# Second branch projection: eight of its sixteen k-tiles as seven products for eight, and two modulation blocks summed by matmuls

## The chip, the cores and the metric

The kernel runs on one core of a Trainium2 chip. The metric is the time of one execution on the device in microseconds (us), the median of several runs; a profile records one more execution, instruction by instruction. The engines are named as in the profile: PE (TensorE, matmuls), PEld (its weight loads), DVE (VectorE), ACT (ScalarE), POOL (GpSimd) and SP (the queue that issues most DMAs).

## The reference, cut to what matters

One layer of a streaming encoder over T = 576 tokens (512 of a prompt, 64 of a sample). What the change touches:

```
mod = (silu(c) @ w_ada + b_ada)                    # 6 blocks of 1024, here cut into 12 of 512 ("u" 0 to 11)
sh1, sc1, gt1, sh2, sc2, gt2 = split(mod, 6)
...
y = group RMSNorm of the Mamba branch              # 576 x 2048
mixed = (g_attn * (o_attn @ w_branch_attn) + g_ssm * (y @ w_branch_ssm)) @ w_out
x = x + gt1 * mixed
h2 = rms_normalize(x) * g_norm_ffn * (1.0 + sc2) + sh2
```

The weights w_branch_attn and w_out are 1024 x 1024, w_branch_ssm is 2048 x 1024, w_ada is 1024 x 6144; all is float32.

## The kernel before

Everything is written once as a list of operations; a planner then places them, engine by engine, by its own table of durations, latencies and a model of the DMA queue, with priorities (`R.prio`), extra caution for matmuls (`R.slack`) and explicit "not before" edges (`R.after`). What it emits is a fixed order per engine, so an engine whose next instruction is not ready waits, whatever stands behind it.

Activations are kept as [128 channels, tokens], and a projection is done for one column tile `a` of 128 outputs at a time. To keep float32 accuracy each operand is split in two: `h` (rounded) by an ACT copy and `l` (the rest) by a DVE subtraction, and each product is three matmuls, wh·yh, wh·yl, wl·yh. One matmul covers 288 tokens (`TH`, half of T). `fm` therefore issues 8 k-tiles x 3 x 2 halves = 48 matmuls for 1024 inputs.

The weights come through `fetch`: a DMA of 512 KB into a `raw` buffer (two of them), then the split into `wh` and `wl` (three slots each). `specs` is the list of weight tiles in the order of use; `getw` takes the next one and lets `fetch` run ahead.

The stage that the change rewrites follows the scan of the Mamba branch. First the attention branch, `pba0` to `pba7` (operands `oh`, `ol`), while the last groups of the scan still run; its gated results go to the DRAM tensor `m_d`. Then the second branch, `pbs0` to `pbs7`: 16 k-tiles `yh`, `yl`, read back from `y_d` through `stage` buffers (`load_split`), 96 matmuls a column tile. Each result is gated (`g`), added to the attention part (`m`, read from `m_d`) and split into `mh`, `ml`. Then comes the output projection `pwo`, on `mh`, `ml`.

Beside this DVE computes modulation blocks 5 to 9 as filler (`ada_columns`): for each block the weights come in four DMAs of 512 KB (tile `adr`), and 32 DVE operations of 512 columns each multiply them by silu(c) and add them up in two accumulators `aacc`, one for the prompt and one for the sample. `ada_sum` then sums over the partitions by 8 small matmuls (`pick`, 32 columns of weights, in four column groups), and `ada_out` turns the result and stores it in `modc`. The blocks of the kernel's very first stage are done another way (`ada_pair`): there the weights go straight through PE, 32 small matmuls a block, `sil` (silu(c)) being the stationary operand. Blocks 10 and 11 come later and stay as they are but for the place of block 10's sum.

The feed-forward projections further on already use the scheme of seven products for eight (Strassen's, in Winograd's form), so the words T1 to T4 (differences of weight quarters) and S1 to S4 (differences of activation quarters) also occur there.

Of the kernel before, what the change touches and what calls it, by code (L numbers as in the profile page):

```python
# [5 lines left out]
F32 = mybir.dt.float32  # L6
F32R = mybir.dt.float32r
# [241 lines left out]
class Plan:  # L249
# [10 lines left out]
    def __init__(self, tc):  # L260
        self.tc, self.nc = tc, tc.nc
        self.ops, self.events, self.offset, self.slack, self.also = [], [], 0, SLACK, []
        self.vec, self.act, self.pool, self.pe, self.sync = (Engine(self, e) for e in ("vector", "scalar", "gpsimd", "tensor", "sync"))
# [25 lines left out]
    def add(self, eng, fn, args, kw):  # L289
# [20 lines left out]
        op.dur, op.dur_dma = self.cost(op, outs, ins)  # L310
        self.ops.append(op)
# [240 lines left out]
def build(tc, I, O):  # L552
# [62 lines left out]
    queue = []  # L615
    state = {"ld": 0, "sp": 0, "get": 0}
    raws, outs, outs_made = {}, {}, []
# [9 lines left out]

    def fetch(done, limit=1 << 30):

        while len(outs_made) < len(specs):  # L630
            i = len(outs_made)
            outs_made.append(i)
            queue.extend((i, s) for s in specs[i])
            outs[i] = []
        with R.prio(4000 if done else 0):
            more = True
            while more:
                more = False
                j = state["ld"]
                if j < min(len(queue), limit) and j < state["sp"] + NRAW:  # L640
                    i, s = queue[j]
                    if s == "misc":
# [4 lines left out]
                    else:  # L647
                        raws[j] = (load_raw(*s), s[1], s[2], 27 <= j < 48)
# [3 lines left out]
                if j < min(state["ld"], limit) and (j < NWH or queue[j - NWH][0] < done):  # L652
                    outs[queue[j][0]].append(split(*raws.pop(j)))
                    state["sp"] += 1
                    more = True
# [87 lines left out]
    def ada(u, pl, bufs):  # L743

        p = px(f"pada{u}", "py")
        raws = [pl.tile([P, 2, 512], F32, name=f"wada{u}_{k2}", tag="adr", bufs=bufs) for k2 in range(4)]
        loads = [sync.dma_start(raw, w_ada[256 * k2:256 * k2 + 256, 512 * u:512 * u + 512].rearrange("(k p) n -> p k n", p=P))
                 for k2, raw in enumerate(raws)]
        with R.after(loads[-1:]):
            for kt in range(8):  # L750
                for g in range(4):
                    pe.matmul(p[32 * g:32 * g + 32, 0:P], sil[:, kt, :], raws[kt // 2][:, kt % 2, P * g:P * g + P],
# [1505 lines left out]
```

## Time and profile before

| | us |
|---|---|
| median of 3 runs (1356.64 to 1356.99) | 1356.81 |
| the profiled execution | 1357.67 |
| span of its instructions, first start to last end | 1355.7 |

The profiled execution lies 1.97 us above its own span and 0.86 us above the median of the runs. A row of a timeline has the start, the time covered, the engine, the operation, what it writes and reads, and a count of equal instructions in a row; in brackets stands the idle time before it and what ended it. A matmul's row lasts longer than the distance to the next start, because matmuls overlap, so costs on PE are read from starts. A plain float32 matmul, as the small ones of the modulation are, leaves two records each, so x16 is 8 of them and x32 is 16.

### The profile page before, as it was taken

To read this page: it belongs to the slowest core of one execution; us is meant where nothing else is said; L and a number is where in the kernel's file an instruction comes from. 1 tells how busy PE (TensorE), PEld (TensorE's weight loads), DVE (VectorE), ACT (ScalarE), POOL (GpSimd) and SP (SyncE) were. 2 spreads that over 40 slices of the span, in tenths; PEclk is the share of its full clock that TensorE was granted. 3 is DMA by queue.
4 is the path that set the end of the run, shared out by engine and by line. 5 is a ranking of instruction groups with operands and counts; after the bars stand their busy time and mean duration, and the time that the engine had idled before them with its cause. 6 is when DMAs were issued, how large, how long until landed. Compare 5 with 4: busy or idle time off the path is not lost.

```text
span 1355.7 us, 27900 instructions
## 1 busy us (share of the span) xinstructions
PE 1341.3 (99%) x10677; PEld 1306.5 (96%) x10677; DVE 1141.8 (84%) x2307; ACT 754.1 (56%) x1593; POOL 245.4 (18%) x377
## 2 busy tenths in 40 slices
PE   7999999999999999999999999999999999999998
PEld 6999999999999999999999999999999999999998
DVE  5788999887778798888887688867799999878897
ACT  5445333777777666666565342225476666665453
POOL 2312011230310235545463300001000000000000
PEclk9999999999999999999999999999999999999999
DMA  9762435574755464454445698747423343325352
GB/s 302 226 181 83 111 107 156 124 186 106 173 136 123 131 180 115 113 150 128 131 124 172 209 294 253 232 141 246 127 87 101 96 131 102 94 74 141 98 164 63
DMA packets 267877, 200.31 MB, mean 148 GB/s; under 512 B 25488, under 2 KB 239616, under 8 KB 267744
## 3 DMA queue, kind: packets, MB, share of 16 engines
q1 hardware_dynamic: 263056, 183.40, 46.3%
q0 software_dynamic: 4400, 15.00, 5.4%
q8 instruction: 83, 1.36, 0.4%
q14 instruction: 50, 0.41, 0.1%
q10 hardware_dynamic: 288, 0.13, 0.0%
HBM read 157.75 MB, written 28.96 MB: 138 GB/s over the span
## 4 chain that ended last, share of the span: by engine, by line
PE 91%; DVE 5%; DMA 1%; issue 1%; ACT 1%; POOL 1%; SPq 0%; DVEq 0%; POOLq 0%; ACTq 0%
PE mm L544 63%; PE py L544 16%; PE px L544 12%; DVE score L544 1%; DVE m L544 1%; DMA raw<-in_w_in 1%; DVE wl L544 1%; DMA bc<-acs_d 0%; DMA B<-in_w_down 0%; SPq L544 0%; DVE tok L544 0%; DVE xs L544 0%; ACT wh L544 0%; DVE rr L544 0%; ACT wl L544 0%
## 5 line engine op out<-in xcount | busy, mean ns | idle before, releaser
L544 ACT ACTIVATE wh<-raw 128x1024 fp32r<-128x1024 f32 (+3 forms) x144 | 140.6, 979 | 172.5 <-PE mm L544 131.6
L544 PE MATMUL mm<-hTl,wh 128*128 128x288 f32 (+1 forms) x1024 | 232.6, 302 | 1.1 <-DVE hTl L544 1.1
L544 PE MATMUL mm<-hTh,wh 128*128 128x288 f32 (+1 forms) x1024 | 231.2, 303 | 0.6 <-ACT wh L544 0.5
L544 PE MATMUL mm<-hTh,wl 128*128 128x288 f32 (+1 forms) x1024 | 230.0, 302 | 0.0
L544 PEld LDWEIGHTS mm<-hTl,wh 128*128 128x128 f32 (+1 forms) x1024 | 166.7, 188 | 4.1 <-DVE hTl L544 1.8
L544 PEld LDWEIGHTS mm<-hTh,wh 128*128 128x128 f32 (+1 forms) x1024 | 165.7, 188 | 3.8 <-ACT wh L544 0.7
L544 PEld LDWEIGHTS mm<-hTh,wl 128*128 128x128 f32 (+1 forms) x1024 | 165.4, 188 | 1.6 <-issue 0.9
L544 DVE TENSOR_TENSOR wl<-raw,wh 128x1024 fp32r<-128x1024 f32 (+2 forms) x99 | 122.1, 1235 | 27.1 <-ACT wh L544 26.0
L544 POOL DMA_DIRECT2D wl<-raw x23 | 20.9, 907 | 471.2 <-PE px L544 312.9
L544 DVE SCALAR_TENSOR_TENSOR cu<-xc,wc,cu 128x579 f32<-128x579 f32 x96 | 83.3, 868 | 2.0 <-ACT cu L544 1.0
L544 PE MATMUL mm<-wh,hTl 128*128 128x256 f32 x256 | 73.2, 286 | 0.0
L544 PE MATMUL mm<-wl,hTh 128*128 128x256 f32 x256 | 72.5, 284 | 0.0
L544 PE MATMUL mm<-wh,hTh 128*128 128x256 f32 x256 | 72.4, 285 | 0.0
L544 DVE SCALAR_TENSOR_TENSOR aacc<-adr,sil,aacc 128x512 f32<-128x512 f32 x84 | 59.0, 751 | 5.0 <-DMA adr<-in_w_ada 4.9
L544 PE MATMUL mm<-yh,wl 128*128 128x288 f32 x256 | 55.2, 296 | 0.0
L544 PE MATMUL mm<-yh,wh 128*128 128x288 f32 x256 | 55.0, 296 | 0.0
L544 PE MATMUL mm<-yl,wh 128*128 128x288 f32 x256 | 54.9, 296 | 0.0
L544 PE MATMUL mm<-xhS,wh 128*128 128x290 f32 (+1 forms) x248 | 54.8, 296 | 0.0
L544 ACT ACTIVATE P<-lg,mn 128x128 f32<-128x128 f32 (+4 forms) x72 | 41.7, 580 | 22.6 <-DVE mn L544 21.3
L544 ACT ACTIVATE dec<-dec,nacs 128x128 f32<-128x128 f32 x128 | 42.4, 393 | 15.9 <-POOL dec L544 15.9
L544 PE MATMUL mm<-xhS,wl 128*128 128x290 f32 (+1 forms) x232 | 51.2, 296 | 0.0
L544 PEld LDWEIGHTS mm<-wh,hTl 128*128 128x128 f32 x256 | 48.3, 189 | 0.4
(565 smaller groups left out, 4071.7 us busy)
## 6 DMA issues: line engine op xcount, KB each, us to landing
raw<-in_w_in SPq DMA_DIRECT2D x80, 512.0 KB, 4.2
adr<-in_w_ada SPq DMA_DIRECT2D x36, 512.0 KB, 5.4
raw<-in_w_gate_up SPq DMA_DIRECT2D x22, 512.0 KB, 3.8
wl<-raw POOLq DMA_DIRECT2D x21, 512.0 KB, 4.7
rawu<-in_w_gate_up SPq DMA_DIRECT2D x20, 512.0 KB, 3.9
bc<-acs_d SPq DMA_DIRECT2D x32, 256.0 KB, 3.7
raw<-in_w_branch_ssm SPq DMA_DIRECT2D x16, 512.0 KB, 4.7
gate_d<-sg SPq DMA_DIRECT2D x16, 288.0 KB, 2.2
```

Of the source, the lines that this page charges most:

```text
L544: getattr(engines[x.eng], x.fn)(*[real(a) for a in x.args], **{k: real(v) for k, v in x.kw.items()})
```

## The change

For k-tiles 0 to 7 of the second branch, the 1024 x 256 weights of two neighbouring column tiles (a pair `r`) and the activations are cut into quarters of 512: B11, B21 (first column tile, k-tiles 0 to 3 and 4 to 7) and B12, B22 (second), A11, A12 (first half of the tokens, k-tiles 0 to 3 and 4 to 7) and A21, A22 (second half). Seven products of 4 k-tiles x 3 = 12 matmuls take the place of eight; they accumulate in banks x, y, z, with copies on ACT and additions on DVE in between. K-tiles 8 to 15 stay as they were (the "plain" part, two column tiles of 48 matmuls a pair). New work on DVE and ACT: the four weight differences of a pair, the four activation differences once, splits of quarters (512 columns of weights, 1152 of activations) in place of whole tiles. Buffers: a pair's two raw tiles stay until their last difference is taken; the plain weights get a `rawp` buffer of their own; S3, S1, A22 and S4 are split into the space of `oh` and `ol` once the attention projection has read them.

Modulation blocks 5 and 6 go through PE as in `ada_pair` (`ada_direct`): four clusters of 16 small matmuls from three `adr` buffers. Blocks 7 to 9 stay on DVE. The gated result is added to `m_d` by an accumulating DMA of POOL's queue for all eight column tiles (`a >= 8` never holds), and `ml` of the first six tiles is made by an ACT copy of -mh and an accumulating DMA.

```diff
@@ fetch @@
+                    if quad is not None and free(tag):
+                        r, q = quad
+                        if n - 2 in raws:
+                            x, y = (raws.pop(n - 2 + k)[0] for k in range(2))
+                            pair_raws[r] = {"B11": x[:, 0:4], "B21": x[:, 4:8], "B12": y[:, 0:4], "B22": y[:, 4:8]}
+                        src = quad_source(r, sum_pool[0], q)
+                        t = wp.tile([P, 8, P], F32R, name=f"wq{q}{r}", tag=tag, bufs=NWH)
+                        act.activation(t[:, 0:4], src, AF.Copy)
+                        vec.tensor_tensor(t[:, 4:8], src, t[:, 0:4].bitcast(F32), OP.subtract)
...
-    for a in range(8):
-        fm_spec(I["w_branch_ssm"][0], P * a, 0)
-        fm_spec(I["w_branch_ssm"][0], P * a, 1024)
+    SSM_ORDER = ((1, 2, 6, 7, 5, 4, 3),) + ((1, 7, 6, 2, 5, 4, 3),) * 3
+    SSM_QUADS = {1: ("B11", "A11"), 2: ("B21", "A12"), 6: ("T2", "S2"), 7: ("T3", "S3"), 5: ("T1", "S1"), 4: ("T4", "A22"), 3: ("B22", "S4")}
+    for r in range(4):
+        pair_spec(I["w_branch_ssm"][0], r, [SSM_QUADS[p][0] for p in SSM_ORDER[r]])
+        for a in (2 * r, 2 * r + 1):
+            fm_spec(I["w_branch_ssm"][0], P * a, 1024)
+            specs[-1][0] += (True,)
...
+    def ada_direct(u, pl, bufs):
+
+        p = px(f"padc{u}", "py")
+        with R.prio(4000):
+            R.slack = 3.0
+            for k4 in range(2):
+                raws = [pl.tile([P, 2, 512], F32, name=f"wada{u}_{k4}{i}", tag="adr", bufs=bufs) for i in range(2)]
...
+                with R.after(loads):
+                    for i in range(4):
+                        for g in range(4):
+                            pe.matmul(p[32 * g:32 * g + 32, 0:P], sil[:, 4 * k4 + i, :], raws[i // 2][:, i % 2, P * g:P * g + P],
...
-    with R.prio(-2000):
-        for u in range(4 + NADX + NADA, 10):
-            ada_columns(u, adv)
...
+    with R.prio(-2000):
+        for u in range(4 + NADX, 10):
+            if u in (5, 6):
+                ada_direct(u, adv, 3)
+            else:
+                ada_columns(u, adv, bank="py", bufs=3)
...
-        ps = fm(f"pbs{a}", getw(2), lambda k: yh[k], lambda k: yl[k])
-        vec.scalar_tensor_tensor(t2(g), t2(g), 1.0, ps, op0=OP.add, op1=OP.mult)
-        vec.tensor_tensor(m, m, g, OP.add)
...
+        if a in mixed:
+            vec.tensor_tensor(g, g, mixed[a], OP.add)
+        else:
+            pool.dma_start(g, m_d[:, a, :], accum_op=OP.add)
...
+        for p in SSM_ORDER[r]:
+            (hi, lo), = getw()
+            o, (yh_q, yl_q), starts = bank["y" if p == 2 else "z" if p in (7, 4) else "x"], yq[SSM_QUADS[p][1]], p in (1, 2, 7)
+            for k in range(4):
+                for w, y in ((hi, yh_q), (hi, yl_q), (lo, yh_q)):
+                    pe.matmul(o, w[:, k], y[:, k], start=(starts and k == 0 and w is hi and y is yh_q), stop=(k == 3 and w is lo),
+                              skip_group_check=not starts)
+            with R.prio(4000):
+                if p in (1, 6, 7):
+                    act.activation({1: acc0[:, :TH], 6: acc0[:, TH:], 7: acc1}[p], o, AF.Copy)
+                if p == 5:
+                    vec.tensor_tensor(acc1, acc1, o, OP.add)
```

Three places show what the planner made of it. In the rows below a name ends in the buffer's number; `mm`, `px`, `py` are PSUM banks.

PE, where the attention projection ends and the second branch begins, before: whole k-tiles, both halves of the tokens in a row.

```order
L544 MATMUL mm_0_114<-ol7_0_5061,wh_1_102 128x288 x2
L544 MATMUL mm_0_114<-oh7_0_5053,wl_1_105 128x288 x2
L544 MATMUL mm_1_115<-yh0_0_9045,wh_2_103 128x288 x2
L544 MATMUL mm_1_115<-yl0_0_9061,wh_2_103 128x288 x2
L544 MATMUL mm_1_115<-yh0_0_9045,wl_2_106 128x288 x2
```

The same engine now, from the end of the first product (A11) on: five matmuls of the product on S3 (in the space of `oh0`), the first of the product on A12, then the second cluster of modulation block 5 (`adr`, 16 small matmuls), then A12 again.

```order
L545 MATMUL mm_1_115<-ylA11_0_9075,wh_2_103 128x288
L545 MATMUL mm_1_115<-yhA11_0_9074,wh_2_103 128x288
L545 MATMUL px_0_112<-oh0_0_5046,wl_0_104 128x288 x5
L545 MATMUL mm_0_114<-yhA12_0_9076,wl_2_106 128x288
L545 MATMUL py_0_110<-adr_2_9050,sil_0_119 32x128 x8
L545 MATMUL py_0_110<-adr_0_9048,sil_0_119 32x128 x8
L545 MATMUL mm_0_114<-ylA12_0_9077,wl_2_106 128x288
L545 MATMUL mm_0_114<-yhA12_0_9076,wl_2_106 128x288 x2
```

So PE's queue now holds matmuls that need a DMA of `w_ada` to have landed, where only DVE needed it before.

PE, some 40 matmuls into the output projection, before: column tile 0 runs through k-tiles 6 and 7, then column tile 1 begins.

```order
L544 MATMUL mm_1_115<-mh6_0_9334,wl_0_104 128x288 x2
L544 MATMUL mm_1_115<-mh7_0_9335,wh_0_101 128x288 x2
L544 MATMUL mm_1_115<-ml7_0_9343,wh_0_101 128x288 x2
L544 MATMUL mm_1_115<-mh7_0_9335,wl_0_104 128x288 x2
L544 MATMUL mm_0_114<-mh0_0_9328,wh_1_102 128x288 x2
```

The same place now.

```order
L545 MATMUL mm_1_115<-mh6_0_9366,wl_0_104 128x288 x2
L545 MATMUL mm_0_114<-mh0_0_9360,wh_1_102 128x288 x2
L545 MATMUL mm_0_114<-ml0_0_9368,wh_1_102 128x288 x2
L545 MATMUL mm_0_114<-mh0_0_9360,wl_1_105 128x288 x2
L545 MATMUL mm_0_114<-mh1_0_9361,wh_1_102 128x288 x2
L545 MATMUL mm_0_114<-ml1_0_9369,wh_1_102 128x288 x2
L545 MATMUL mm_0_114<-mh1_0_9361,wl_1_105 128x288 x2
L545 MATMUL mm_0_114<-mh2_0_9362,wh_1_102 128x288 x2
L545 MATMUL mm_0_114<-ml2_0_9370,wh_1_102 128x288 x2
L545 MATMUL mm_0_114<-mh2_0_9362,wl_1_105 128x288 x2
L545 MATMUL mm_0_114<-mh3_0_9363,wh_1_102 128x288
L545 MATMUL mm_1_115<-mh7_0_9367,wh_0_101 128x288 x2
```

Nineteen matmuls of column tile 1 were moved ahead of k-tile 7 of column tile 0, so 42 + 19 = 61 matmuls stand before the first use of `mh7`, where 42 did.

DVE in the middle of the stage, before: gating, one weight split of 1024 columns, the addition of the attention part, modulation.

```order
L544 SCALAR_TENSOR_TENSOR g_1_9348<-g_1_9348,mm_0_114 128x576
L544 TENSOR_TENSOR wl_2_106<-raw_1_100,wh_2_103 128x1024
L544 TENSOR_TENSOR m_1_9350<-m_1_9350,g_1_9348 128x576
L544 SCALAR_TENSOR_TENSOR aacc0_0_9038<-adr_1_9041,sil_0_119,aacc0_0_9038 128x512
L544 SCALAR_TENSOR_TENSOR aacc1_0_9039<-adr_1_9041,sil_0_119,aacc1_0_9039 128x512
L544 TENSOR_TENSOR ml1_0_9337<-m_1_9350,mh1_0_9329 128x2x256
```

DVE in the middle of the stage now: one quarter's split (`wh_1`), T1, T2 and T3 of the next pair with modulation between them, T3's split (`wl_1`), the plain weights' split, the additions out of banks y and z.

```order
L545 TENSOR_TENSOR wh_1_102<-raw_1_100,wh_1_102 128x512
L545 TENSOR_TENSOR raw_0_99<-raw_0_99,raw_1_100 128x512
L545 SCALAR_TENSOR_TENSOR aacc1_0_9052<-adr_2_9050,sil_0_119,aacc1_0_9052 128x512
L545 TENSOR_TENSOR T2b_0_9047<-raw_0_99 128x512
L545 SCALAR_TENSOR_TENSOR aacc0_0_9051<-adr_2_9050,sil_0_119,aacc0_0_9051 128x512
L545 TENSOR_TENSOR raw_1_100<-T2b_0_9047,raw_1_100 128x512
L545 SCALAR_TENSOR_TENSOR aacc1_0_9052<-adr_2_9050,sil_0_119,aacc1_0_9052 128x512
L545 TENSOR_TENSOR wl_1_105<-raw_1_100,wl_1_105 128x512
L545 TENSOR_TENSOR wl_0_104<-rawp_0_9046,wh_0_101 128x1024
L545 TENSOR_TENSOR acc0_0_9053<-acc0_0_9053,mm_1_115 128x288
L545 TENSOR_TENSOR acc0_0_9053<-acc0_0_9053,px_1_113 128x288
```

The `m` additions and most `ml` subtractions have left DVE; weight differences, more and shorter splits and additions out of PSUM have come to it.

## Rows read from the trace of the kernel before

**Rows 1.** The page, busy time by engine, and the granted clock in 40 slices.

```profile
PE 1341.3 (99%) x10677; PEld 1306.5 (96%) x10677; DVE 1141.8 (84%) x2307; ACT 754.1 (56%) x1593; POOL 245.4 (18%) x377
...
PEclk9999999999999999999999999999999999999999
```

**Rows 2.** Waits of PE over the whole run: total us, times, longest.

```profile
PE py L544 <- POOL ident L544: 1.7, 1, 1.7
...
PE py L544 <- DVE xwS L544: 0.5, 1, 0.5
```

**Rows 3.** Busy time by stretch: PE, PEld, DVE, ACT, POOL, clock, DMA share, GB/s.

```profile
785.40:804.60 19.20, 19.20 (x146) 19.20 (x146) 18.41 (x28) 11.49 (x17) 0.00 (x0) 1.00 0.94 300
804.60:910.90 106.30, 106.30 (x855) 104.49 (x854) 85.11 (x134) 24.38 (x34) 1.60 (x6) 1.00 0.72 226
```

**Rows 4.** PE's timeline, second branch, around a modulation sum, and its end.

```profile
804.66 0.42 PE L544 MATMUL mm<-yh,wh 128*128 128x288 f32 x2
...
818.25 0.43 PE L544 MATMUL mm<-yh,wh 128*128 128x288 f32 x2
818.62 0.64 PE L544 MATMUL px<-aacc,pick 128*32 128x128 f32 x16
819.19 0.53 PE L544 MATMUL mm<-yl,wh 128*128 128x288 f32 x2
819.56 0.42 PE L544 MATMUL mm<-yh,wl 128*128 128x288 f32 x2
...
910.91 0.43 PE L544 MATMUL mm<-mh,wh 128*128 128x288 f32 x2
```

**Rows 5.** PE's timeline in the first stage, around half a modulation block.

```profile
28.57 0.29 PE L544 MATMUL mm<-hTl,wh 128*128 128x288 f32 x1
28.80 1.08 PE L544 MATMUL py<-adr,sil 128*32 128x128 f32 x32
29.81 0.40 PE L544 MATMUL mm<-hTl,wh 128*128 128x288 f32 x1
30.05 0.43 PE L544 MATMUL mm<-hTh,wl 128*128 128x288 f32 x2
```

**Rows 6.** DVE's groups by form, 785 to 912 us: busy us, mean ns, idle before.

```profile
L544 DVE SCALAR_TENSOR_TENSOR aacc<-adr,sil,aacc 128x512 f32<-128x512 f32 x70 | 48.5, 744 | 1.0 <-DMA adr<-in_w_ada 0.9
L544 DVE TENSOR_TENSOR wl<-raw,wh 128x1024 fp32r<-128x1024 f32 x19 | 23.2, 1219 | 8.6 <-ACT wh L544 8.5
L544 DVE TENSOR_TENSOR yl<-stage,yh 128x576 fp32r<-128x576 f32 x14 | 10.1, 753 | 0.5 <-ACT yh L544 0.5
...
L544 DVE TENSOR_TENSOR m<-m,g 128x576 f32<-128x576 f32 x8 | 6.0, 756 | 0.2
L544 DVE TENSOR_TENSOR ml<-m,mh 128x512 fp32r<-128x512 f32 x7 | 4.8, 682 | 0.0
```

**Rows 7.** A DVE addition out of PSUM, 288 columns, from the whole run's groups.

```profile
L544 DVE TENSOR_TENSOR gg<-gg,mm 128x288 f32<-128x288 f32 x6 | 2.7, 446 | 0.0
```

**Rows 8.** DMAs issued from 765 to 912 us: count, KB each, median us to landing.

```profile
adr<-in_w_ada SPq DMA_DIRECT2D x20, 512.0 KB, 4.5
raw<-in_w_branch_ssm SPq DMA_DIRECT2D x16, 512.0 KB, 4.7
stage<-y_d SPq DMA_DIRECT2D x14, 288.0 KB, 5.9
```

**Rows 9.** Landing of all w_ada loads of SP, whole run, us.

```profile
DMA to landing us min/median/max: 2.8/4.9/10.2
```

**Rows 10.** Landing of POOL's accumulating DMAs of 512 KB, whole run, us.

```profile
DMA to landing us min/median/max: 3.9/4.7/7.0
```

**Rows 11.** DVE's timeline at the end of the stage, and ACT's copies to mh.

```profile
911.11 0.76 DVE L544 SCALAR_TENSOR_TENSOR g<-g,mm 128x576 f32<-128x576 f32 x1 [4.31 <-PE mm L544]
...
913.71 0.82 DVE L544 TENSOR_TENSOR ml<-m,mh 128x512 fp32r<-128x512 f32 x2
...
L544 ACT ACTIVATE mh<-m x16: 238/437/637, 819.2 to 913.2; 128x512 fp32r<-128x512 f32 x8, 128x64 fp32r<-128x64 f32 x8
```

More of the change, by code (lines that the diff above doesn't have):

```diff
@@ L614, in build @@
     specs = []
[L615 to L617 removed]
+    loads, preps = [], []
+    state = {"ld": 0, "sp": 0, "get": 0, "half": 0}
+    raws, outs, outs_made, slots, pair_raws = {}, {}, [], {"wh": [], "wl": []}, {}
     def fm_spec(w, c0, r0=0):
@@ L741, in build @@
     sh1, sc1, gt1, sh2, sc2, gt2 = (modc[:, i] for i in range(6))
[L743 to L752, printed above, removed]
-                              start=(kt == 0), stop=(kt == 7), tile_position=(0, 32 * g))
-        ada_out(u, p)
     pairs_bank = px("padp", "py")
@@ new lines, in build @@
+    yh, yl = ({k: yh_p.tile([P, T], F32R, name=f"y{n}{k}") for k in range(8, 16)} for n in "hl")
+    yq = {q: [yh_p.tile([P, 4, TH], F32R, name=f"y{n}{q}") for n in "hl"] for q in ("A11", "A12", "S2")}
+    src = {}
+    for i, q in enumerate(("A11", "A12", "A21", "A22")):
+        with R.prio(1500):
+            src[q] = gtp.tile([P, 4, TH], F32, name=f"yr{q}")
+            R.reserve = 2
+            sync.dma_start(src[q], y_d[:, 4 * (i % 2):4 * (i % 2) + 4, TH * (i // 2):TH * (i // 2) + TH])
+            R.reserve = 0
@@ new lines, in split_y @@
+    def split_y(q, v):
+        with R.prio(4000):
+            keep_split(v, *yq[q])
+    src["S2"] = gtp.tile([P, 4, TH], F32, name="yrS2")
+    with R.prio(1500):
+        vec.tensor_tensor(src["A21"], src["A11"], src["A21"], OP.subtract)
+        vec.tensor_tensor(src["S2"], src["A22"], src["A21"], OP.subtract)
+    split_y("A11", src["A11"])
+    with R.prio(1500):
+        vec.tensor_tensor(src["A11"], src["A11"], src["S2"], OP.add)
+    split_y("A12", src["A12"])
+    with R.prio(1500):
+        vec.tensor_tensor(src["A12"], src["A12"], src["S2"], OP.subtract)
@@ L1611, in build @@
+    split_y("S2", src["S2"])
+    for k in range(8, 16):
         if k < 14:
-            load_split(gtp, y_d[:, k, :], yh[k], yl[k], 4)
+            load_split(gtp, y_d[:, k, :], yh[k], yl[k], 3)
         else:
             keep_split(ykeep[k - 14], yh[k], yl[k])
-    R.close(gtp)
+    for q, v, o in (("S3", src["A21"], "h0"), ("S1", src["A11"], "l0"), ("A22", src["A22"], "h1"), ("S4", src["A12"], "l1")):
+        t = op_.tile([P, 2, 4, TH], F32R, name="y" + q, tag="o" + o)
+        yq[q] = [t[:, 0], t[:, 1]]
+        with R.prio(4000):
+            split_y(q, v)
```

158 lines of the change are left out of this document (127 added, 31 removed).

## The prediction

> **What bounds the kernel now.** I read the busy times first. PE is busy for 1341.3 of 1355.7 us, at the full granted clock in every slice [rows 1]. Next come the waits of PE: the longest of the run is 1.7 us, at the start, and the last scan groups cost it 0.5 us beside the attention projection [rows 2]. Last I read the stage by stretch. In the 19.2 us before the second branch and in its 106.3 us, PE is busy for every microsecond; DVE works 18.41 and 85.11 us, 82% together, and ACT less [rows 3]. So in this stage the time is the sum of what PE issues. A microsecond of matmuls taken away shortens the run by a microsecond as long as weights, activations and banks still come in time, and a microsecond taken from DVE alone is worth nothing.
>
> This gives three questions: what PE issues less, what it issues more, and whether anything makes it wait.
>
> **PE issues less.** Per pair of column tiles the plain half keeps 96 matmuls, and seven products of 12 take the place of 96: 180 in place of 192. Over four pairs 768 become 720, so 48 matmuls of 288 columns go. Their price is the distance between starts. From 804.66 to 818.25 us 51 rows of two make 13.59 us, 133 ns each. Over the whole stage, 804.66 to 910.91, five modulation sums at 0.78 (next paragraph) and five turnings at about 0.13 leave 106.25 - 3.9 - 0.65 = 101.7 us for 768, 132 ns each [rows 4]. The new products are the same instruction with the same width, so I take 0.1325 us: **-6.4 us**, between 6.3 and 6.5.
>
> A rule speaks against that size. The Trainium skill ("TensorE: Matmul & The Clock Gate", section "Back-to-back issue gap") gives an isolated gap of columns over 2.4 GHz plus 2.5 ns. For 288 columns this is 122.5 ns, as an estimate from that page, and 48 of them would be 5.9 us. The rows here have 133 ns, in pairs with their weight loads, so the measured price stands.
>
> **PE issues more.** A modulation sum is 8 small matmuls (x16 in records). The pair of matmuls ahead of one starts at 818.25 and would be done issuing at 818.52; the pair behind it starts at 819.19 and takes until 819.56, 0.10 us longer than its 0.27. So one cluster costs 819.56 - 0.27 - 818.52 = 0.78 us, changing over there and back included [rows 4]. Blocks 5 and 6 lose theirs: -1.56 us. In their place come four clusters of 16 small matmuls, for which the first stage has the same shape (x32). One matmul at 28.57 would be done at 28.70; the one at 29.81 and its follower at 30.05 show that the cluster ends at 30.05 - 0.13 = 29.92: 1.21 us [rows 5]. Four of them are +4.86 us. The turning of each result stays. Net **+3.3 us**; the lowest and highest that the two rows allow, with 0.05 us a cluster either way, are 3.0 and 3.6.
>
> The balance of PE's work is -6.4 + 3.3 = **-3.1 us**.
>
> **Edits that cost nothing if their cover holds.** The copies of banks x and z and the additions out of PSUM (0.45 us each [rows 7]) stand beside matmuls into the other banks; gone is that cover only where a bank is wanted again at once, and by the written order the next use is 12 matmuls (1.6 us) or more away. The weight differences and splits run ahead of PE: after a pair's last difference its two raw buffers are free, 12.8 us of plain products before the next pair needs anything, against 4.7 us of landing [rows 8] and some 3 us on ACT and DVE. The activations A11, A12 and S2 are split while the attention projection runs. S3 must wait until its column tile 7 has read `oh` k-tiles 0 to 3, 24 matmuls or 3.2 us before its end; an ACT copy and a DVE subtraction of 1152 columns follow. DVE's rows have 1.22 us for 1024 columns and 0.75 for 576 [rows 6], so 1.3 to 1.5 us; with S1 ahead of it about 1 us is left until S3's first matmul, 12 behind the end. That is tight, but it is covered.
>
> DVE's load: it loses 32 operations of modulation (-21), eight splits of 1024 (-9.8), eight additions of m (-6.0), six tiles' `ml` (-5.4) and eight `yl` (-5.8), 48 us. It gains 28 splits and 16 differences of 512 at 0.69 (+30), seven splits and four differences of 1152 at 1.4 (+15), some 16 operations out of PSUM at 0.45 in place of gatings (+6 to 7), 52 us [rows 6, 7]. So 103.5 us become about 108 of 122: 88%.
>
> **Waits that are new.** PE's queue now holds matmuls on `adr`. Block 5's second cluster reads a buffer that the first cluster frees. The first stands 34 matmuls ahead of the attention projection's end and the second 18 behind it, so from that load's issue to its use 52 matmuls and half of each cluster pass, about 8 us. These loads landed in 4.9 us as the median and 4.5 in this stretch, but in 10.2 at the worst [rows 8, 9]. Behind a waiting cluster stands everything on PE. The other two clusters have 8 to 10 us. At the median nothing waits; at the worst one cluster waits 2.2 us. I take 0.
>
> At the end of the stage the attention part comes by an accumulating DMA. From the last matmul: 0.3 us until DVE starts [rows 11], one addition and two gatings of 288 columns (1.3), the DMA (3.9 to 7.0 for 512 KB, median 4.7; here it is 288 KB [rows 10]), two ACT copies (0.64 + 0.24 [rows 11]): 7.2 us at the median. The first use of `mh7` is 61 matmuls away, 8.1 us. Before it was 42, 5.6 us. So 0 at the median and 1.4 us at the worst; I take 0.2 for all waits together, being nearest to the medians.
>
> **Sum.** -6.4 + 3.3 + 0.2 = -2.9 us on the profiled execution, 1357.67 to 1354.8. The median of the runs lies 0.86 us below that execution, so **1353.9 us** against 1356.81. What a measurement of this kernel can tell from no change is about 0.2%, 2.7 us, so this forecast lies on that edge: below 1354.1 counts as faster.
>
> **Rivals.**
>
> *Late loads (w_ada for a cluster, or a quarter's weights).* For it: the DMA share is 0.94 ahead of the stage [rows 3], and the loads of blocks 5 and 6 now come in a bunch there. Against it: the weights' loads landed in 4.7 us [rows 8], and the same bytes were moved before. One or two waits of 0.5 to 2.2 us: 1354.4 to 1356.5, within 0.2%.
>
> *The accumulating DMA is late at the end.* For it: landings up to 7.0 us [rows 10]. Against it: fewer bytes, and a stretch with little other traffic. Up to 1.4 us: 1355.1, within 0.2%. The Trainium skill ("SBUF — State Buffer", section "Who interferes with whom") says that a DVE operation in a two-port mode locks GpSimd out while it prepares such DMAs, and that subtractions of two tensors have no such mode. By that rule the splits that run there would not delay it; no run here shows it.
>
> *DVE paces the middle pairs: slower.* A pair now needs 7 splits and 4 differences of 512 (7.6), 2 splits of 1024 (2.4), 4 additions and the gatings (3.3), and one block of modulation (10.6), about 24 us, where PE's 180 matmuls and one sum need 24.6. It decides where DVE's idle time, 22 us of 125.5 in the stage before [rows 3] or 4.3 per pair, can't shrink below 0.6. If it stays in three pairs, each is 3.7 us longer: +11 - 3.1, 1364.8; if half of it stays, +1.5 a pair, +4.6 - 3.1 = +1.5, 1358.3. From 1.9 us a pair on (1359.5) the kernel is measurably slower. Against it: over two fifths of that work is modulation, whose result PE turns only when it is done, and before, DVE waited because it was ahead (8.5 us for ACT's halves of splits [rows 6]).
>
> **How the numbers follow.** All covered, waits under 0.4 us: 0.55, 1353.4 to 1354.1. Late loads: 0.22. Late accumulation: 0.10. DVE as the pace: 0.13, of which 0.08 end over +0.2%. Below 1354.1 lies nearly all of the first case and none of the others: faster 0.53, same 0.38, slower 0.09. The range reaches from the sum with all bounds in favour (-6.5 + 3.0 = -3.5, and 0.5 for the wait of [rows 2], if the changed order removes it: 1352.8) up to 1356.8, where both kinds of late DMA together would end.
>
> **What would show each step.** 720 matmuls at 0.13 us and the stage some 3 us shorter; four clusters x32 costing 1.2 us each; no row of PE's waits in the stage over 0.5 us. Wrong: a wait of PE on `adr`, `wh`, `wl` or `mh` of a microsecond or more, most likely at block 5's second cluster or at the first `mh7`; or DVE without idle time while PE waits for its splits.

## The result, and the profile after

The changed kernel is slower: 1366.28 us (1362.59 to 1371.21, 6 runs) against 1357.38 beside it, a ratio of 1.0069 with a 95% interval of 1.0047 to 1.009, about 9 us. The forecast was 2.9 us in the other direction. The profiled execution took 1366.01 us, its span 1364.3.

From the page: PE's busy time and the granted clock, to be held against [rows 1].

```profile
PE 1343.3 (98%) x10725; PEld 1305.6 (96%) x10725; DVE 1144.2 (84%) x2314; ACT 770.6 (56%) x1636; POOL 269.8 (20%) x397
...
PEclk9999999999999999999999999999999999999999
```

PE is busy 2 us longer, but the span grew by 8.6: most of the loss is time in which PE stands. The waits of PE over the whole run (answers to [rows 2]):

```profile
PE py L545 <- DVE ra L545: 1.9, 2, 1.0
PE py L545 <- DMA adr<-in_w_ada: 1.8, 2, 1.1
...
PE py L545 <- DVE xw L545: 1.6, 1, 1.6
PE px L545 <- DVE dec L545: 1.3, 1, 1.3
...
PE mm L545 <- ACT acc L545: 1.0, 2, 0.6
```

`adr`, `ra` and `acc` belong to the rewritten stage. `xw` and `dec` belong to the scan, which the change was not meant to touch. The next table says where the time went; each mark is the start of a matmul in the two traces.

| stretch | before | after | difference |
|---|---|---|---|
| scan: first `xw` to first matmul of the attention projection | 480.85 to 738.41: 257.56 | 480.96 to 743.87: 262.91 | +5.35 |
| from there to the first matmul of the second branch | 66.25 | 69.12 | +2.87 |
| second branch, to the first `mh` | 106.25 | 106.17 | -0.08 |
| output projection | 53.33 | 53.30 | -0.03 |

The rest, 0.5 us, lies ahead of the scan (0.1) and further on (0.4). The scan of before is that of its first profile; in every later run with the old order it takes 256.6 or 256.7 us, so against those the loss is 6.3. The two middle stretches by engine (answers to [rows 3]):

```profile
743.87:812.99 69.12, 67.30 (x581) 63.78 (x580) 50.34 (x86) 30.26 (x52) 14.01 (x15) 1.00 0.80 253
812.99:919.16 106.17, 103.29 (x872) 99.85 (x870) 83.67 (x139) 37.94 (x73) 20.76 (x19) 1.00 0.86 220
```

PE was busy for every microsecond of [rows 3]; now it stands for 2.9 us in the second branch, although DVE has no more to do than before (83.67 us against 85.11). PE's timeline of that stage, the places of [rows 4]:

```profile
806.50 0.65 PE L545 MATMUL py<-adr,sil 128*32 128x128 f32 x16 [1.12 <-DMA adr<-in_w_ada]
807.79 0.65 PE L545 MATMUL py<-adr,sil 128*32 128x128 f32 x16 [0.65 <-DMA adr<-in_w_ada]
...
812.99 0.30 PE L545 MATMUL mm<-yhA,wh 128*128 128x288 f32 x1
...
908.78 0.33 PE L545 MATMUL py<-ident,ra 128*128 128x128 f32 x1 [0.98 <-DVE ra L545]
...
919.16 0.43 PE L545 MATMUL mm<-mh,wh 128*128 128x288 f32 x2
```

Adding up distances between starts, the 720 wide matmuls take 101.06 us where 768 took 103.25, and the small ones 5.11 where they took 3.0. In the 101.06 are four stops of PE (at `acc` and `ra`) that last 3.5 us more than an ordinary step. The chain of waits in this stage shows what stands behind them (start, duration, what):

```profile
856.91 5.77 DMA ml<-g
...
862.82 2.78 DMA g<-gate_d
...
870.41 7.00 DMA g<-m_d
877.43 0.64 ACT mh L545
...
879.84 6.91 DMA ml<-g
886.89 2.85 DMA g<-gate_d
...
890.92 4.91 DMA g<-m_d
...
898.15 7.51 DMA g<-m_d
...
906.22 1.05 ACT wh L545
907.30 1.23 DVE wl L545
908.52 0.21 DVE ra L545
908.78 0.33 PE py L545
```

ACT's rows at that place show the link between the transfer and the weight split:

```profile
905.69 0.63 ACT L545 ACTIVATE mh<-g 128x512 fp32r<-128x512 f32 x1 [5.73 <-DMA g<-m_d]
906.22 1.04 ACT L545 ACTIVATE wh<-raw 128x1024 fp32r<-128x1024 f32 x1
```

ACT stands 5.73 us at `mh`, because the accumulating DMA that adds the attention part into `g` has not landed (it adds `m_d` into `g`, not the gated result into `m_d`, as the part on the change has it). Behind it in ACT's queue is a weight split; DVE waits for that split, behind it stands the small copy `ra`, and PE stands at the turning of `ra` with all its matmuls behind. ACT waits for these transfers 20.1 us in six waits. The Trainium skill ("TensorE: Matmul & The Clock Gate", section "Architectural detail: the array is 16× 32×32, not 1× 128×128") says that ACT and DVE take their queues strictly in order; these rows agree.

### The profile page after: what moved, and what is told of

Its sections match the earlier page's. It is cut to its first block, busy times and chain, and to the rows that moved or that the text cites. A ratio compares the mean times of both kernels' runs of the same rounds, so it can differ in the third digit from the quotient of the medians.

```text
span 1364.3 us, 28080 instructions
## 1 busy us (share of the span) xinstructions
PE 1343.3 (98%) x10725; PEld 1305.6 (96%) x10725; DVE 1144.2 (84%) x2314; ACT 770.6 (56%) x1636; POOL 269.8 (20%) x397
## 5 line engine op out<-in xcount | busy, mean ns | idle before, releaser
L545 ACT ACTIVATE wh<-raw 128x1024 fp32r<-128x1024 f32 (+3 forms) x140 | 130.9, 938 | 120.7 <-PE mm L545 96.7
L545 DVE TENSOR_TENSOR wl<-raw,wh 128x1024 fp32r<-128x1024 f32 (+2 forms) x83 | 102.2, 1233 | 16.0 <-ACT wh L545 14.9
L545 PE MATMUL mm<-xhS,wh 128*128 128x290 f32 (+1 forms) x248 | 54.8, 296 | 0.0
L545 PEld LDWEIGHTS mm<-wh,hTh 128*128 128x128 f32 x256 | 48.1, 188 | 0.6 <-issue 0.4
L545 PEld LDWEIGHTS mm<-wl,hTh 128*128 128x128 f32 x256 | 48.3, 189 | 0.2
L545 DVE CUSTOM_DVE_ANT_0 lg<-py,mask 128x128 f32<-128x128 f32 (+4 forms) x72 | 33.9, 483 | 15.3 <-PE py L545 15.2
L545 POOL TENSOR_TENSOR cs<-bc,bcx 128x512 f32<-128x512 f32 (+1 forms) x32 | 42.3, 1323 | 12.4 <-ACT bc L545 9.4
```

The source lines that it names most:

```text
L545: getattr(engines[x.eng], x.fn)(*[real(a) for a in x.args], **{k: real(v) for k, v in x.kw.items()})
```

## The experiments

All 18 runs; times in us. The stretches are those of the table above, each from that run's trace. The kernel before took 1355.9 to 1357.0 beside them. The second branch ends at the first `mh`; in e4 and e7, 44 of its 720 wide matmuls come only after that mark, so some 5.9 us (44 at 134 ns) stand under the projection there.

| run | time | ratio to before, 95% | scan | to 2nd branch | 2nd branch | output proj. |
|---|---|---|---|---|---|---|
| e12 before again | 1357.41 | | 256.6 | 66.0 | 106.2 | 53.3 |
| changed kernel | 1366.28 | 1.0069 (1.0047 to 1.009) | 262.9 | 69.1 | 106.2 | 53.3 |
| e1 before, o_d loads planned longer | 1360.07 | 1.0028 (1.0017 to 1.0039) | 259.9 | 65.6 | 106.2 | 53.3 |
| e2 change, scan order back | 1360.67 | 1.0037 (1.0023 to 1.005) | 256.6 | 68.1 | 106.0 | 54.0 |
| e3 e2, transfers planned longer | 1368.77 | 1.0097 (1.0082 to 1.0112) | 256.6 | 68.0 | 111.0 | 58.9 |
| e4 e2, blocks 5, 6 on DVE | 1373.55 | 1.0128 (1.0111 to 1.0145) | 256.6 | 65.7 | 101.0 | 74.6 |
| e5 before, blocks 5, 6 by matmuls | 1360.37 | 1.003 (1.0018 to 1.0041) | 256.6 | 66.0 | 109.8 | 53.3 |
| e6 e2 without m (the attention part is missing from the result) | 1355.49 | 0.9997 (0.9988 to 1.0007) | 256.6 | 71.6 | 102.1 | 53.3 |
| e7 e2, three slacks | 1363.44 | 1.0056 (1.0042 to 1.007) | 256.6 | 66.8 | 104.0 | 60.0 |
| e8 e2, ra later | 1359.56 | 1.0033 (1.002 to 1.0046) | 256.6 | 69.6 | 103.3 | 54.7 |
| e9 e2, m by loads, DVE adds | 1379.01 | 1.0163 (1.0149 to 1.0177) | 256.6 | 68.9 | 117.9 | 61.3 |
| e10 e2, w_ada loads planned longer | 1364.90 | 1.0059 (1.0047 to 1.0072) | 256.6 | 67.1 | 107.1 | 60.8 |
| e11 e9 and e10 | 1371.45 | 1.0116 (1.0097 to 1.0135) | 256.6 | 66.8 | 119.3 | 54.8 |
| e13 e2, four buffers of g | 1368.86 | 1.0089 (1.0075 to 1.0102) | 256.6 | 68.5 | 104.6 | 64.5 |
| e14 e13, transfers planned longer | 1368.72 | 1.0092 (1.0078 to 1.0105) | 256.7 | 69.5 | 102.1 | 65.2 |
| e15 e2, tail as before | 1368.73 | 1.0087 (1.0073 to 1.01) | 256.6 | 68.7 | 100.3 | 66.6 |
| e16 e2, ml on DVE | 1359.36 | 1.002 (1.0011 to 1.0029) | 256.6 | 69.0 | 107.2 | 53.6 |
| e17 e16, ra later | 1364.87 | 1.0066 (1.0043 to 1.0088) | 256.7 | 69.2 | 106.4 | 57.0 |
| e18 e17, w_ada 1 us longer | 1357.36 | 1.0003 (0.9994 to 1.0011) | 256.6 | 67.4 | 103.7 | 54.6 |

### The scan's order: e1, e2, e12

`load_split` was given two microseconds more in the planner's account of its loads. It is used for `y_d` in the rewritten stage, and for `o_d` in the middle of the scan. e1 makes this edit in the kernel before, for `o_d` alone; e2 takes it out of the changed kernel there; e12 is the kernel before.

```diff
 e1 (kernel before)
+        R.reserve = 2 if pl is sd else 0
         sync.dma_start(o, src)
+        R.reserve = 0
 e2 (changed kernel)
-        R.reserve = 2
+        R.reserve = 2 if pl is not sd else 0
         sync.dma_start(o, src)
```

> The kernel before with one edit: the planner counts 2 us more for the loads of the attention output (o_d) that run inside the scan. By the orders, every engine's row order from the start of the scan up to the last scan group is then that of the changed kernel. Theory A (the changed order of the scan loses time by itself: in the changed kernel's profile the first attention-projection matmul comes 5.5 us and the last decay matmul 5.0 us later than before): slower by 4 to 6 us, about 1362.4 us against 1357.4, with the first projection matmul near 744 in place of 738.4. Rival B (the stalls at 613 and 665 us come from loads that landed late in that one execution): within 1 us of before. Rival C (the scan is slowed by what runs beside it only in the changed kernel): within 1 us of before.

> The changed kernel with the 2 us taken off the o_d loads again and kept on the y_d loads: the scan has the order of before, all else is the change. Theory A: 1366.3 - 5.2 = 1361.1 us (1360 to 1362.5), the first projection matmul back near 738.5, and a narrower spread of the runs. Rivals B and C: 1365 to 1367. In either case the rest of the loss, about 1.8 us of waits on w_ada at the first sums and 2.9 us on late copies of block sums and banks, stays.

> The kernel before, unchanged, for its profile on the chip of these runs. Its first profile took 1357.67 us, the runs beside the experiments 1355.9 to 1356.5. The difference should lie ahead of the scan or be spread over it, and the second branch should again take 106.2 us within 0.2.

e1 is 4.1 us slower than before, and its scan takes 259.9 us; in every run here with the old order, whatever came after it, it takes 256.6 or 256.7 (257.6 in the first profile of before). e2 gains what the two ratios differ by, 0.32% or 4.3 us. Theory A holds for 3.3 us of the scan; the first projection matmul of e1 comes at 741.9, not near 744. For this part B and C fall, since e1 has nothing else of the change and stops at the same `xw` for the same 1.59 us as the changed kernel. In e1 it is this chain, on SP, POOL, DVE and PE in turn:

```profile
653.83 0.53 SPq L545 DMA_DIRECT2D bc<-acs_d  x1
...
659.36 0.43 POOL L545 TENSOR_SCALAR_AFFINE_SELECT decS<-bc 64x256 f32<-64x256 f32 x1 [5.66 <-DMA bc<-acs_d]
...
661.39 1.23 DVE L545 TENSOR_TENSOR wl<-raw,wh 128x1024 fp32r<-128x1024 f32 x1 [1.87 <-ACT wh L545]
662.77 0.42 DVE L545 TENSOR_TENSOR xw<-px,wst 128x256 f32<-128x256 f32 x1
...
663.25 0.70 PE L545 MATMUL py<-xw,bt 128*128 128x256 f32 x2 [1.59 <-DVE xw L545]
```

In the kernel before, the same sixth `decS` waited for the same load like this:

```profile
654.03 0.74 POOL L544 TENSOR_SCALAR_AFFINE_SELECT decS<-bc 64x256 f32<-64x256 f32 x1 [1.13 <-DMA bc<-acs_d]
```

In SP's new order the load was issued 3.7 us later and landed after 5.5 us in place of 3.8; POOL stood for it, ACT's split stood behind POOL's result, `xw` stood behind that split on DVE.

In the changed kernel's profile one more stop, of 1.3 us at `dec` near 613 us, came on top, and e1's profile has none there. SP, POOL and DVE take the same rows in the same order around it in both. But POOL's row took longer in the changed kernel, 2.57 us where e1's took 1.20, and DVE waited for POOL, which it did not in e1:

```profile
608.29 2.57 POOL L545 TENSOR_SCALAR_AFFINE_SELECT dec<-bc 128x512 f32<-128x512 f32 x1 [2.90 <-DMA bc<-acs_d]
...
612.26 0.69 DVE L545 TENSOR_TENSOR dec<-dec,px 128x512 f32<-128x512 f32 x1 [1.90 <-POOL dec L545]
```

So the order alone does not make this stop, and B and C stay open for it.

### One part of the change alone: e5, e4

e5 puts only blocks 5 and 6 through PE in the kernel before; e4 keeps only the seven products (on e2).

```diff
 e5 (kernel before)
-            ada_columns(u, adv)
+            if u in (5, 6):
+                ada_direct(u, adv, 2)
+            else:
+                ada_columns(u, adv, bank="py")
 e4 (on e2)
-            if u in (5, 6):
+            if u in ():
```

> The kernel before with the second part of the change alone: blocks 5 and 6 summed by matmuls from w_ada, the plain second branch kept. DVE loses 32 operations, which it does not need here, PE gains four clusters at 1.21 us for two at 0.78. If the price of a cluster is what the first stage showed and the loads come in time: +3.3 us, 1359.2 us against 1355.9. If PE also waits for w_ada as in the changed kernel (1.1 to 1.8 us): 1360.3 to 1361. If the clusters are hidden or cheaper than read: under 1358.

> As the second run, and blocks 5 and 6 are summed on DVE again (32 operations of 0.69 us, 22 us, and two clusters of PE at 0.57 to 0.78 us in place of four at 1.0 to 1.9). PE alone would gain 3.3 us and the two waits on w_ada, 1.8 us: 1356 us if DVE has room. Theory E (DVE is full in the middle quarters, with 4 us idle in 54): it has not, the waits on ra and wl grow, and the time is 1361 to 1366. If it ends under 1359, DVE was not the limit and ACT's order was.

e5 costs 3.85 us (1360.37 against 1356.52 beside it), with 3.3 forecast for the clusters, and its second branch grows by 3.5 us: that price holds. e4 shows that the seven products, in the order that the planner found, lose more without this part. PE's stops at `ra` in the second branch grow from 1.6 to 3.35 us, with none at `wl`. The last block's sum comes at 933.4, long after the first `mh` at 903.9; PE stops 6.8 us for it, and the output projection takes 74.6 us, 68.7 without the 44 matmuls that moved there. That is theory E, though most of the loss lies behind the stage, where I did not expect it. (The 32 operations are those of both blocks: a block is 16 in the traces, 48 for the three that stay on DVE, not 32 as the part on the kernel before has it.)

### ACT behind the transfer of m: e6, e3

```diff
 e6 (on e2)
-            pool.dma_start(g, m_d[:, a, :], accum_op=OP.add)
+            pass
 e3 (on e2)
-        op.dur_dma += self.reserve if eng == "sync" else 0
+        op.dur_dma += self.reserve if eng == "sync" or fn == "dma_start" else 0
...
+            R.reserve = 3
             pool.dma_start(g, m_d[:, a, :], accum_op=OP.add)
+            R.reserve = 0
...
+                R.reserve = 3
                 pool.dma_start(t2(ml[a])[:, :, d0:d0 + dn], src, accum_op=OP.add)
```

> The changed kernel with the scan's order of before (second run), and the accumulating transfers of the attention part m_d into g left out: the attention branch is missing from the sum, nothing stands in its place. Theory D (ACT stands at mh for these transfers, 25.3 us in the second run's profile, and the weight splits and bank copies behind it make DVE's ra and PE late): the waits of PE on ra and acc, 2.7 us, go, 1360.7 - 2.7 = 1358.0 us (1357.3 to 1358.8). Theory E (DVE is full in the middle quarters, whatever ACT does): less than 0.8 us changes, 1360 to 1361.5.

> As the run before it, and the planner counts 3 us more for the two kinds of accumulating transfers (attention part into g, and g into ml), so that it places ACT's copies of mh later; no instruction is added or removed. Theory D (ACT stands in its queue at mh, waiting for the transfer of m_d: 20.1 us in six waits in the changed profile, and what is queued behind it, weight splits and bank copies, makes DVE's copy of ra and PE late): the four waits of PE on ra and acc, 2.9 us, go, and the time falls by 2 to 3 us, to about 1358.5. Rival E (DVE is full in the middle quarters, 25.5 and 24.4 of 27 us, and would be late anyway): less than 0.8 us changes, 1360.5 to 1361.5.

Without the transfer the second branch takes 102.1 us, in the profile from the first row here to the second:

```profile
809.21 0.29 PE L545 MATMUL mm<-yhA,wh 128*128 128x288 f32 x1
...
911.29 0.43 PE L545 MATMUL mm<-mh,wh 128*128 128x288 f32 x2
```

That is 4.2 us less than before. Of PE's waits from the scan on only these are left:

```profile
PE py L545 <- DMA adr<-in_w_ada: 3.0, 2, 2.3
PE py L545 <- ACT yo L545: 0.4, 1, 0.4
```

Those on `ra` and `acc` are gone, and the kernel gains 5.2 us on e2, twice what D expected, although in its profile the stretch before (71.6 us) got longer by the waits on `adr` and by a granted clock of 0.50 for 3.4 us behind them. D is right about the transfer, with one limit: e6 was planned anew, so its gain is that of the transfer together with the order around it. e3 then shows that the obvious repair, to plan for it, makes things worse by 8 us. ACT's waits at `mh` fall from 25.3 to 6.0 us, and PE waits elsewhere:

```profile
PE mm L545 <- DVE g L545: 4.6, 2, 3.3
PE mm L545 <- ACT acc L545: 2.7, 2, 2.5
```

DVE's `g` in turn waits 6.7 us for `g<-gate_d`. There are two buffers of `g`, each held from the gate's load to the landing of the transfer into `ml`; a later `mh` holds them longer. This is the cycle that the chain of waits above runs through twice. Behind e3's two longest stops, 2.5 and 3.3 us, the granted clock is 0.50 for 3.4 us each.

### Matmuls placed later on PE: e8, e10, e7

```diff
 e8 (on e2; also in e7)
+        R.slack = 3.0 if u >= 5 else SLACK
         pe.transpose(p2[:, 0:P], ra, ident)
+        R.slack = SLACK
 e10 (on e2; also in e7)
+                R.reserve = 4
                 with R.prio(-6000):
...
+                R.reserve = 0
                 with R.after(loads):
 e7: both, and
-        R.slack = 0.8
+        R.slack = 2.0
         for p in SSM_ORDER[r]:
```

> As the second run, and only the turning of ra stands 3 us later in the planner's account. Theory F: the two waits on ra, 1.6 us, go, 1359.1 us (1358.5 to 1359.7). Rival: the order of all that follows is replanned, other waits come, 1360 or more.

> As the second run, and the planner counts 4 us more for the w_ada loads of blocks 5 and 6, so that PE meets these clusters later. If the wait on w_ada (1.1 us in the second run's profile, 1.8 to 3.0 in others) is only a cluster placed too early: -1.1 to -2.5 us, 1358.2 to 1359.6. If the clusters' later place brings ra and what follows later too: 1360 to 1362.

> As the second run, and the planner is told that three things come later: the loads for blocks 5 and 6 by 4 us, ra for its turning by 3 us, the bank copies by 2.0 us in place of 0.8. No instruction is added or removed; PE meets these matmuls later in its queue. Theory F (the 3.8 us of waits on w_ada, ra and acc are PE standing in its queue at matmuls that were placed too early, with other work behind them): they go and nothing takes their place, 1357 to 1358.5 us. Rival (the run with 3 us more for the accumulating transfers went up by 8 us: buffers and banks are so tight that a wait put off comes back elsewhere): 1360 to 1369, with waits on g, wh or the banks.

e8 wins 1.1 us of the 1.6 by the medians and 0.5 by the ratios, which is inside the noise; in its profile the waits on `ra` are gone, and those on `adr` have grown to 2.5. e10 takes the waits on `adr` away and is 4 us slower all the same; e7 is 3 us slower. Theory F falls for both. In e7 the wait comes back at a bank, as the rival had it, and behind its 3.1 us the granted clock is 0.50 for 3.4 us:

```profile
PE mm L545 <- ACT acc L545: 4.1, 2, 3.1
```

The 60.0 us of e7's projection are no loss there: they hold the 44 wide matmuls of the second branch (5.9 us) and one block sum (0.7) more. In e10 the stops at `acc` grow from 1.1 to 2.6 us; in its projection, which has one block sum more, PE stops 2.9 us at `mh` and `ml`, with a clock of 0.50 for 3.4 us behind them.

A mark that no expectation had named moved in both: the cluster that sums the last modulation block, here by the start of its last matmul. In e10 that is at 921.8 and in e7 at 916.2, after the first `mh` (911.6 and 908.6); in the changed kernel it is at 906.0, 13 us ahead of the first `mh`. PE does not stop at this cluster in either run, so that its late place costs these two anything is not shown.

### The tail on DVE again, and more buffers: e9, e11, e13, e14, e15

```diff
 e9 (on e2; e11 with e10's edit)
-            pool.dma_start(g, m_d[:, a, :], accum_op=OP.add)
+            for h in range(2):
+                mt = mxt.tile([P, TH], F32, name=f"m{a}{h}", tag="m", bufs=1)
+                R.reserve = 3
+                sync.dma_start(mt, m_d[:, a, h * TH:h * TH + TH])
+                R.reserve = 0
+                vec.tensor_tensor(g[:, h * TH:h * TH + TH], g[:, h * TH:h * TH + TH], mt, OP.add)
 e13 (on e2; e14 with e3's edit)
-                ada_direct(u, adv, 3)
+                ada_direct(u, adv, 2)
...
-                ada_columns(u, adv, bank="py", bufs=3)
+                ada_columns(u, adv, bank="py", bufs=2)
...
-            gates[a] = mxt.tile([P, T], F32, name=f"gs{a}", tag="g", bufs=2)
+            gates[a] = mxt.tile([P, T], F32, name=f"gs{a}", tag="g", bufs=4)
 e15 (on e2, "adr" in two buffers as in e13)
-            if a >= 8:
+            if a >= 0:
...
-            if a < 6:
+            if a < 0:
```

> As the second run, but the attention part comes as before by plain loads (in halves, one buffer, for space) and DVE adds it: no accumulating transfer into g, 16 additions of about 0.45 us on DVE. Theory D (ACT's wait at mh was the cause in the second branch; with the part left out the stage took 102.1 us, 4.2 less than before): 1360.7 - 2.7 to -4 = 1356.7 to 1358 us, less up to 1 us more if DVE's 7 us find no room. Rival (DVE is full, as with blocks 5 and 6 on it): 1361 or more. The waits on w_ada stay.

> Both edits of this call together, all on the scan's old order: if they add up, 1354 to 1356 us against 1355.9 to 1356.5 of before, the stage near 102.5 us and no wait of PE on acc, ra or adr over 0.5 us. That would be the forecast's balance of PE's work (-3.1 us, here from 1356.2: 1353.1) less what is left. If waits move instead of going: 1358 or more.

> As the second run, with four buffers for g in place of two (adr has two in place of three to make room). Nothing else is edited. Theory G (g is held from the gate's load until the transfer into ml has landed, and late loads follow): the waits on ra and acc shrink, the stage goes from 106.0 to 103 or 104 us, 1358 to 1359 us. Theory D (ACT stands at mh for the transfer of m_d whatever the buffers): no change, 1360 to 1361.5; waits on w_ada may add up to 2 us in either case, since adr has a buffer less.

> As the run before it, and the planner counts 3 us more for the accumulating transfers, which with two buffers of g made the kernel 8 us slower (third run: PE waited 4.6 us for DVE's g behind late loads of gate_d). Theory G with D (the later place of mh was right and only the buffers were missing): the waits on ra, acc and g go, the stage takes 102 to 103 us, 1356 to 1358 us. If it is again slower than the run before by 2 us or more, the buffers of g were not what the third run lacked.

> As the second run, with the whole tail of a column tile as before: m comes by a plain load into two buffers of its own, DVE adds it and makes ml, no accumulating transfer (adr has two buffers). DVE gets 8 additions of 0.75 and six tiles' ml of about 0.9, 11.4 us, on 83.7 busy of 106. Theory E (DVE is full in the middle quarters, 51 of 54 us): 1365 to 1375, with PE waiting for wl, ra and acc. Theory G (buffers and transfers, not DVE's sum, were short): 1356.5 to 1359.

All five are much slower, in two ways. In e9 and e11 the addition waits for a half of `m` with one buffer, gate loads come late, and PE stands at a bank that DVE has not emptied. The longest such stop of e11, 6.5 us, follows the transfer into `ml` (6.95 us) and the gate load that waited for it. In e9:

```profile
PE mm L545 <- DVE g L545: 12.5, 3, 6.0
```

In e13, e14 and e15 the second branch is short: 104.6, 102.1 and 100.3 us, with one or two block sums moved out of it (0.7 us each). So more buffers (G), together with planning for the transfer (D), do cure the stage, as expected (e14); the buffers alone bring little, 104.6 + 0.7 against e2's 106.0 (e13). But the last cluster comes at 928.1, 926.9 and 927.6, some 17 to 21 us after the first `mh`. In the projection PE stops 6.7 to 8.2 us at `aacc` and `ra`, the granted clock is 0.50 for 10.2 us, and the projection takes 64.5 to 66.6 us. In e15, PE's stops there:

```profile
926.75 1.31 PE L545 MATMUL py<-aacc,pick 128*32 128x128 f32 x16 [6.17 <-DVE aacc L545]
930.12 0.48 PE L545 MATMUL py<-ident,ra 128*128 128x128 f32 x1 [2.06 <-DVE ra L545]
```

The projection's results are added to `x`, and scaled by `A2`, which is made from `sc2`, the product of blocks 8 and 9. So the sums of these blocks are due soon after the projection starts, and DVE does them last, as filler. In e13 to e15 `adr` had a buffer less, in e10 and e7 it was held longer; that this is why the sums came late is read from the orders and was not tried by itself.

### The version that comes nearest: e16, e17, e18

```diff
 e16 (on e2)
-            if a < 6:
+            if a < 0:
 e17 (on e16)
+        R.slack = 3.0 if 5 <= u < 10 else SLACK
         pe.transpose(p2[:, 0:P], ra, ident)
 e18 (on e17): e10's edit with 1 in place of 4
```

> As the second run, with only ml of the first six tiles on DVE again (two subtractions, 0.9 us, a tile; ACT loses two copies a tile and g comes free at once instead of 5 to 8 us later). The transfer of m_d into g stays. Theory G: g is free earlier, the waits on ra and acc shrink, 1358 to 1359.5. Theory E: 5.4 us more for DVE make 1362 to 1366.

> The changed kernel with the scan's old order, ml of the first six tiles on DVE, and ra counted 3 us later for its turning. If PE's stand at ra (0.8 us) and what follows it is all that this can win: 1358 to 1359 us against 1359.4 for ml on DVE alone. The last cluster should come before the first mh and the output projection take 53.3 to 54.5 us. It beats the kernel before (1356 to 1357) only if the waits on wl, adr and the low clock after them also go, 1355 to 1356.5.

> As the run before it, and the planner counts 1 us more for the w_ada loads of blocks 5 and 6. The wait on adr (1.1 to 3.0 us) shrinks by about 1 us; everything that adr holds comes later, the last modulation block too. Theory H (the last block's cluster against the start of the output projection decides): if the cluster still comes before the first mh, 1357 to 1358.5 us; if it comes after it, the projection takes 58 us or more and the time is 1361 to 1366.

With `ml` on DVE a buffer of `g` comes free without the second transfer; e16 is at 1359.36, inside G's range, though its interval overlaps that of e2. e17 missed: 5.5 us slower than e16 instead of 1 us faster, with a projection of 57.0 us although the last cluster is in time (903.8 against 913.7). A stop at `mh` there (1.6), with a granted clock of 0.50 for 3.4 us behind it, makes up most of the excess; the stops at `wl` (1.4) and `wh` (1.0) lie in the second branch. I tested no cause of these stops. e18 is at 1357.36, no different from before. All waits of PE from the scan on in its profile:

```profile
PE mm L545 <- ACT acc L545: 0.8, 1, 0.8
PE py L545 <- ACT yo L545: 0.4, 1, 0.4
PE py L545 <- DMA adr<-in_w_ada: 0.4, 1, 0.4
```

The last matmul of its last cluster starts at 910.3, behind the first `mh` at 909.2, and the projection takes 54.6 us, not the 58 or more that theory H had for that: the cluster's place alone does not decide. e18 also keeps the transfer of `m`, and of the stops behind it one of 0.8 us is left, so that transfer need not cost what e6 gained. So the 9 us come back, but the forecast's 3 do not: against e12 the stretch before the second branch takes 1.5 us more (one cluster at 1.2, the wait at `adr`), the second branch 2.6 less, and the projection 1.2 more, of which a block sum that moved there is about 0.7.

## Why the prediction was wrong

**PE issues less, PE issues more: right.** Without stops (e6) the 720 wide matmuls take 97.19 us, 135 ns each, where 768 took 103.25, 134 ns each; that is 6.1 us of the 6.4 (5.7 in the changed kernel, its stops taken off). The small matmuls of the stage grew by 2.1 us, where three clusters at 1.21 for two at 0.78 make 2.07, and e5 measured 3.85 us for four against the 3.3. The stage that follows from the forecast's terms, 106.25 - 6.4 - 2 x 0.78 + 3 x 1.21 = 101.9 us, is the one that e6 shows (102.1).

**"Edits that cost nothing if their cover holds": the step that failed.** I listed the instructions of the rewritten stage, but not the edit to the planner's account in `load_split`, which issues nothing. It serves the scan too, and the new order of the scan costs 4.1 us by e1, 4.3 by e2. No term and no rival of the forecast had it.

The second failure is in the same step. I took `m` and `ml` off DVE and counted POOL's transfers only at the end of the stage. There, no wait came, so the second rival did not happen. But each of eight column tiles has a transfer, 4.9 us as the median in this stage and up to 7.5 in the chain above, and ACT stands in its queue for it with weight splits and bank copies behind. "Waits that are new: 0.2 us" was 3.5 us of stops in this stage beside 1.8 at `adr`, and e6 gives 5.2 us for the transfer with all that was planned around it.

**Late loads: the rival came true as well.** I took 0 for the clusters of block 5. The first of them waited twice, for each of its two buffers, 1.12 and 0.65 us, within the 0.5 to 2.2 of the rival; it was the block that I had named, but not its second cluster. The w_ada loads took 6.1 us as the median around this stage where I had read 4.5 [rows 8].

**DVE as the pace.** The changed kernel doesn't show it: from 19.2 us ahead of the second branch to its end DVE works 101.5 us, where before it had 103.5 and I had forecast 108. Part of that forecast was mis-read: by [rows 6] the 32 operations come to some 22 us (48.5 for 70), not 21. But e4 shows how near it is, and that the price is paid elsewhere than I put it (so does e15, though with a buffer of `adr` less): not 3.7 us a pair in the middle, but all at once when the last block's sum is late for the output projection.

The sum of the parts: +5.35 in the scan, or 6.3 against the 256.6 of the later runs, of which 3.3 is the order as e1 shows it (259.9 against 256.6) and 3.1 what the changed kernel has over e1, the further stops at and behind `dec` (1.3 and 0.5) and some 1.1 by the low clock behind them (below); +2.87 for one cluster and two waits on `adr`; in the stage -6.4 + 2.1 + 3.5 leave -0.8, measured -0.08. Of the 0.7 between them, 0.65 are longer steps of wide matmuls: 22 of 0.19 to 0.24 us where the kernel before has 15.

## What to carry to other kernels

Where a planner fixes the order of every engine, an edit to its durations is a change like any other: compare the orders over the whole program, not over the stage that was rewritten, and price each stretch that moved. Work taken off a busy engine by a transfer costs nothing only if nothing is queued behind whoever waits for the transfer: look for the first instruction that reads its result, on which engine it stands, and what stands behind it. Filler work has a due time: before a stage is made denser, find what needs the filler's last result, since e4 and e13 to e15, where that result came late, stopped PE for 6.7 to 8.2 us there.

## What the runs showed of the hardware

A stop of PE cost more than its length. After the stop of 1.3 us at `dec` and one of 0.48 behind it, the granted clock of the changed kernel fell to half for 3.4 us (busy times, then clock, DMA share, GB/s):

```profile
611.00:613.00 2.00, 0.70 (x13) 0.40 (x9) 0.74 (x2) 2.00 (x6) 1.03 (x5) 1.00 0.87 226
613.00:615.00 2.00, 1.51 (x10) 1.28 (x11) 1.20 (x5) 2.00 (x5) 1.53 (x2) 1.00 0.38 114
615.00:617.00 2.00, 2.00 (x10) 1.91 (x10) 1.48 (x3) 1.62 (x6) 1.30 (x2) 0.53 0.40 113
617.00:618.50 1.50, 1.50 (x8) 1.41 (x7) 1.02 (x3) 0.00 (x0) 1.43 (x2) 0.50 0.44 99
618.50:620.50 2.00, 2.00 (x17) 2.00 (x17) 0.93 (x2) 0.00 (x0) 0.16 (x1) 0.99 0.39 117
```

0.50 is 1.2 in place of 2.4 GHz: most steps between wide matmuls are 0.24 us there and 0.13 behind. The 13 steps from 615.04 on take 3.40 us; in e1, where the same matmuls follow at a clock of 1.00, they take 2.29, so some 1.1 us are lost without a wait in any list. The stops of up to 1.12 us around the second branch left the clock at 1.00, and so did the 1.59 us at `xw`. The same 1.59 us at `mh` in e17, with 0.19 behind it, was followed by 0.50 for 3.4 us, and in e15 it is 0.50 from 925 to 935 us, from within the stop of 6.17 on. So the length of a stop alone does not tell what follows it. The Trainium skill ("TensorE: Matmul & The Clock Gate", section "Part 1: The HAM clock gate (the "warmup" mystery)") says that the low clock is the default and that activity releases it; these rows agree. The spread of the changed kernel's runs goes with the clock: their mean granted clock is 0.999 in the shortest (1362.59 us) and 0.996 to 0.998 in the others.
